# Hybrid decoder block: first weight parts of a group queued earlier, down inputs split in pieces, one weight ring to the end

## The chip, the cores and the metric

The kernel runs on one core of a Trainium2 chip. The metric is the device time of the whole program in microseconds (us). The core has a matrix engine (TensorE, PE in the profile; its weight loads are PEld), VectorE (DVE), ScalarE (ACT), GpSimd (POOL), and SyncE (SP), which here issues most of the DMA transfers.

## The reference, cut to what matters

One decoder block on 256 tokens of width 2048: a mixer (pooling beside differential attention), an output projection with a norm, then a dense SwiGLU feed-forward with D_FF = 5632, whose projections are the part that the change touches. All is float32.

```python
proj = rms_norm(h, pre_mix_norm) @ w_in
mixed = concat([pool_out, attn_out]) @ w_out
h = h + rms_norm(mixed, post_mix_norm)

hn = rms_norm(h, pre_ffn_norm)
ff = (silu(hn @ w_gate) * (hn @ w_up)) @ w_down
h = h + rms_norm(ff, post_ffn_norm)
```

## The kernel before, in words

**Precision.** Every float32 product is made of three matmuls in a reduced float32 format. Each operand is split into a high part (a rounding copy, on ACT) and a low part (operand minus high part, on DVE), and high x high, low x high and high x low are summed in PSUM. So each piece of weights that SP loads (`raw`) has to be split by one ACT instruction (`whi`, `wh`, `rh`) and one DVE instruction (`wlo`, `wl`, `rl`) before PE can use it in full.

**Feed-forward, first half.** The 5632 columns are done in 11 groups of 512 (index c). Group 0 is done with plain products: `w_g0`, then `w_u0`. Groups 1 to 10 are one loop. Its step j (0 to 7) takes a tile of 1 MB that holds two k-slices of w_up and of w_gate (`blocks`, two transfers). In steps j of `SK = (0, 2, 5)` the 2 x 2 blocks are multiplied with seven products in place of eight, which needs four sums of weight blocks: DVE makes `T` with three instructions (line 697), and `rh`, `rl`, `wh`, `wl` are the parts of the blocks and of the sums. The other steps only split the tile. Behind step 5 the banks m1, m5, m6 and m7 are combined into `s1`, `u2`, `u3`, `u4` (tag `cmb`, eight buffers in the pool `ft`). Behind step 7 come the evacuations: DVE makes `sg` from m2 and m4, ACT applies SiLU, DVE makes `u` from m3 and m8, and `gated` makes the two tiles `gg`. These are transposed on PE in `g_parts` of the next group (line 675, through one PSUM bank, tag `m5`) and copied to `gT[c]` by ACT (line 676).

**Down projection.** `closing` runs over four chunks of 512 output columns; each goes over k = 0 to 43 (tiles of four k, two halves of 512 KB). Its left operands are the split `gT`: `gh` on ACT (line 781), `gl` on DVE (line 782), one instruction each for a group's four k, made in chunk 0 ahead of k = 0, 4, 8 and so on. At the end of a chunk the sum of squares is taken on ACT and the gain is applied on DVE into a tile `mg`. In the last chunk the last eight k are held back and done for the first 128 tokens, then for the other 128. The residual `x` is read back from DRAM (`kept`).

**Memory.** The pools of the left and right side of the SBUF are stacks. The loop over groups has its weight ring `ring2` on the right (`raw` three tiles of 1 MB, `wh` and `wl` two, `rh` and `rl` two, `T` one). After the loop it closes `ring2`, the activations `acts`, `psum_m` and `ft`, and opens `last` and `ring3` in their place. `ring3` has six raw halves and five halves of each part.

**Order.** The program is written in the order of the source. A planner, when the program is built, runs its own model of time and hands each engine the instruction that the model finds ready; of several ready ones it takes the earlier in the source. `tc.issue_after(i)` keeps an instruction behind i on i's engine. On the chip every engine works through its list in the planned order and waits where an input is not ready. With `reuse_waits="tile"` a tile waits only for the tiles whose memory it takes over.

These lines stand around the change (before):

```python
gg = [gated(ps[t][:, :], t) for t in range(2)]      # group 0, ahead of the loop
...
raw = blocks(j)                                      # in step j of the loop
...
g_parts(NF // 4 - 1, gg)                             # behind the loop
p_ring2.close(); p_acts.close(); p_m.close(); p_ft.close()
...
before_k[0] = lambda c, i: g_split(i // 4) if c == 0 and i % 4 == 0 else None
```

Of the kernel before, what the change touches and what calls it, by code (L numbers as in the profile page):

```python
# [15 lines left out]
P = 128  # L16
S = 256
D = 2048
# [27 lines left out]
def block_kernel(ctx: ExitStack, tc: tile.TileContext, x, xT, pos, cols, rows, lamv, invf, invcnt,  # L46
# [4 lines left out]
    cp = ctx.enter_context(tc.tile_pool(name="cp", bufs=1))  # L51
    p_acts = ExitStack()
    acts = p_acts.enter_context(tc.tile_pool(name="acts", bufs=1, side="right"))
    p_ring = ExitStack()
# [10 lines left out]
    def small(shape, dt=F32, tag="tiny", bufs=24):  # L65
        return tiny.tile(shape, dt, tag=tag, name=nm(tag), bufs=bufs)
# [9 lines left out]

    def raw_tile():
        return ring.tile([P, 1024], F32, tag="raw", name=nm("raw"), bufs=RAW)
# [3 lines left out]
    def load(src, half):  # L82
        raw = raw_of[0]()
        latest[0] = sync.dma_start(raw, src[:, half * 1024:(half + 1) * 1024]).ins
        return raw
# [9 lines left out]
    parts_of = [lambda raw: ring_parts()]  # L95

    def split(raw, parts=None, by=None):
        hi, lo = parts() if parts else parts_of[0](raw)
        act.activation(hi, raw, AF.Copy)  # L99
        (by or dve).tensor_tensor(lo, raw, hi.bitcast(F32), ALU.subtract)  # L100
        return hi, lo
# [122 lines left out]

    pad = small([P, 8], tag="pad", bufs=1)
    pool.memset(pad, 0.0)
# [403 lines left out]
    ft = p_ft.enter_context(tc.tile_pool(name="ft", bufs=1, reuse_waits="tile"))  # L630
    p_m = ExitStack()
    psum_m = p_m.enter_context(tc.tile_pool(name="psum_m", bufs=1, space=bass.MemoryType.PSUM, reuse_waits="tile"))

# [23 lines left out]
    p_ring.close()  # L657
    p_ring2 = ExitStack()
    ring2 = p_ring2.enter_context(tc.tile_pool(name="ring2", bufs=1, side="right", reuse_waits="tile"))

    def gated(up, t):
        res = ft.tile([P, 512], F32, tag="gg", name=nm("gg"), bufs=3)
        dve.scalar_tensor_tensor(res, up, rstd3[:, t:t + 1], sg[t], ALU.mult, ALU.mult)
        return res

    gg = [gated(ps[t][:, :], t) for t in range(2)]

# [9 lines left out]

    def blocks(j):
# [22 lines left out]
    cmb = lambda name: ft.tile([P, 512], F32, tag="cmb", name=nm(name), bufs=CMB)  # L701

    for c in range(1, NF // 4):
        src = w_gu[c - 1]
        m = {1: bank(), 2: bank(), 3: bank(), 4: bank(), 5: None, 6: bank2(), 7: psum_m.tile([P, 512], F32, tag="m7", name=nm("m7"), bufs=1), 8: bank2()}
# [13 lines left out]

        for j in range(NKD // 2):  # L720
            raw = blocks(j)
            k1, k2 = 2 * j, 2 * j + 1
            if j in SK:
                if m[5] is None:
                    m[5] = m5_bank()
                s = ring2.tile([P, 4, 512], F32, tag="T", name=nm("T"), bufs=1)
                rh = high(raw[:, 1:4], "rh")
                tt(s[:, 0:2], raw[:, 1:3], raw[:, 0:1].to_broadcast([P, 2, 512]), ALU.add)
                tt(s[:, 2], s[:, 0], raw[:, 2], ALU.add)
                tt(s[:, 3], s[:, 2], raw[:, 3], ALU.add)  # L730
                rl = low(raw[:, 1:4], rh, "rl")
                sh = high(s, "wh")
                sl = low(s, sh, "wl")
                form = lambda i: (sums_h[j][:, i], sums_l[j][:, i])
                product(1, hh(k1, 0), rh[:, 0], rl[:, 0])
                product(3, form(3), rh[:, 1], rl[:, 1])
                product(2, hh(k2, 0), rh[:, 2], rl[:, 2])
                product(7, form(1), sh[:, 1], sl[:, 1])
                product(6, form(2), sh[:, 2], sl[:, 2])
                product(4, hh(k2, 1), sh[:, 3], sl[:, 3])  # L740
                product(5, form(0), sh[:, 0], sl[:, 0])
            else:
                wh = high(raw, "wh")
                wl = low(raw, wh, "wl")
# [12 lines left out]
        sg = [cp.tile([P, 512], F32, tag="gain", name=nm("sg"), bufs=2) for _ in range(2)]  # L757
        for t, (i, u) in enumerate(((2, s1), (4, u3))):
# [15 lines left out]
    raw_of[0] = lambda: ring3.tile([P, 1024], F32, tag="raw", name=nm("raw"), bufs=RAW)  # L774
    parts_of[0] = lambda raw: [ring3.tile([P, 1024], F32R, tag=f"w{z}", name=nm(f"w{z}"), bufs=5) for z in ("hi", "lo")]
    gh, gl = [], []

    def g_split(c):
        gh.append(last.tile([P, 4, 2, P], F32R, name=f"gh{c}"))
        gl.append(fp.tile([P, 4, 2, P], F32R, tag="g", name=f"gl{c}", bufs=NF // 4 + 1))  # L780
        act.activation(gh[c], gT[c], AF.Copy)
        dve.tensor_tensor(gl[c], gT[c], gh[c].bitcast(F32), ALU.subtract)

    mg_tile = lambda: last.tile([P, 512], F32, tag="mg", name=nm("mg"), bufs=8)
    for t in range(2):
        xn[t] = last.tile([P, D], F32, name=f"x{t}")
        load_after(xn[t], kept[t])
    f_k = (lambda k, t: gh[k // 4][:, k % 4, t, :], lambda k, t: gl[k // 4][:, k % 4, t, :])
    before_k[0] = lambda c, i: g_split(i // 4) if c == 0 and i % 4 == 0 else None

# [63 lines left out]
```

## Time and profile before

| | us |
|---|---|
| median of 3 runs | 1064.86 (1064.5 to 1066.73) |
| the profiled execution | 1064.52 |
| its span, first to last instruction | 1062.7 |
| PE busy | 1031.5 (97%) |
| DVE busy | 735.2 (69%) |
| ACT busy | 541.8 (51%) |
| mean granted clock of PE | 0.988 |

A row of a time line has the start in us from the span's start, the duration, the engine, the line of the source, the operation, output <- inputs with shapes, and the count where neighbours are merged; in square brackets stands the idle time of the engine before it and what ended it. A row of waits reads: who waited <- for whom: us in total, times, longest. A row of a costly group has, after the count, busy us and the mean in ns of one, then the idle time before them and what ended it. A row of transfers has the size of one and the us from issue to landing. A matmul's busy time overlaps with the next one's, so the spacing of starts tells its cost, not the mean of one.

### The profile page before, as it was taken

To read this page: it belongs to the slowest core of one execution; us is meant where nothing else is said; L and a number is where in the kernel's file an instruction comes from. 1 tells how busy PE (TensorE), PEld (TensorE's weight loads), DVE (VectorE), ACT (ScalarE), POOL (GpSimd) and SP (SyncE) were. 2 spreads that over 40 slices of the span, in tenths; PEclk is the share of its full clock that TensorE was granted. 3 is DMA by queue.
4 is the path that set the end of the run, shared out by engine and by line. 5 is a ranking of instruction groups with operands and counts; after the bars stand their busy time and mean duration, and the time that the engine had idled before them with its cause. 6 is when DMAs were issued, how large, how long until landed. Compare 5 with 4: busy or idle time off the path is not lost.

```text
span 1062.7 us, 12625 instructions
## 1 busy us (share of the span) xinstructions
PE 1031.5 (97%) x4787; PEld 846.2 (80%) x4787; DVE 735.2 (69%) x836; ACT 541.8 (51%) x632; POOL 35.1 (3%) x57
## 2 busy tenths in 40 slices
PE   8999999999999899999999999999986999999996
PEld 6789888988777688888888888888875888888885
DVE  6649755865677778888888788897867454444544
ACT  6746555654638455544555455555546343343431
POOL 0003100200030000000000000000000000000000
PEclk9999999999999899999999999999997999999999
DMA  8753554555755355665555555556537655655542
GB/s 330 279 175 131 180 179 160 166 188 192 253 191 179 113 197 185 206 212 177 197 198 198 198 198 183 202 191 216 179 129 276 213 194 188 199 196 192 197 139 79
DMA packets 57517, 203.39 MB, mean 191 GB/s; under 512 B 6896, under 2 KB 7792, under 8 KB 56688
## 3 DMA queue, kind: packets, MB, share of 16 engines
q1 hardware_dynamic: 57168, 202.44, 55.7%
q8 instruction: 37, 0.61, 0.2%
q14 instruction: 24, 0.20, 0.1%
q10 hardware_dynamic: 288, 0.15, 0.0%
HBM read 198.37 MB, written 4.19 MB: 191 GB/s over the span
## 4 chain that ended last, share of the span: by engine, by line
PE 87%; DVE 4%; DMA 4%; ACT 2%; issue 1%; SPq 0%; DVEq 0%; ACTq 0%
PE mm L136 14%; PE mm L135 14%; PE mm L137 14%; PE mm L716 8%; PE mm L718 8%; PE mm L717 8%; PE tr L717 3%; PE tr L716 3%; PE tr L718 3%; PE mm L171 2%; PE mm L173 1%; PE mm L172 1%; PE m L716 1%; PE m L717 1%; PE m L718 1%
## 5 line engine op out<-in xcount | busy, mean ns | idle before, releaser
L100 DVE TENSOR_TENSOR wlo<-raw,whi 128x1024 fp32r<-128x1024 f32 x185 | 226.7, 1227 | 190.8 <-ACT whi L99 184.3
L99 ACT ACTIVATE whi<-raw 128x1024 fp32r<-128x1024 f32 x185 | 195.0, 1058 | 212.4 <-PE mm L136 194.4
L135 PE MATMUL mm<-whi,gh 128*128 128x512 f32 x352 | 140.3, 399 | 2.7 <-ACT whi L99 2.7
L136 PE MATMUL mm<-whi,gl 128*128 128x512 f32 x352 | 140.5, 399 | 0.0
L137 PE MATMUL mm<-wlo,gh 128*128 128x512 f32 x352 | 137.1, 391 | 0.0
L717 PE MATMUL mm<-wh,h 128*128 128x512 f32 x330 | 129.4, 392 | 0.0
L716 PE MATMUL mm<-wh,h 128*128 128x512 f32 x330 | 129.3, 392 | 0.0
L688 DVE TENSOR_TENSOR wl<-raw,wh 128x2048 fp32r<-128x2048 f32 x50 | 114.3, 2286 | 6.7 <-ACT wh L693 6.7
L718 PE MATMUL mm<-wl,h 128*128 128x512 f32 x330 | 113.3, 393 | 0.0
L688 DVE TENSOR_TENSOR wl<-T,wh 128x2048 fp32r<-128x2048 f32 x30 | 68.7, 2289 | 54.7 <-ACT wh L693 54.7
L693 ACT ACTIVATE wh<-T 128x2048 fp32r<-128x2048 f32 x30 | 57.4, 1913 | 95.4 <-DVE T L697 69.3
L693 ACT ACTIVATE wh<-raw 128x2048 fp32r<-128x2048 f32 x50 | 95.4, 1908 | 13.7 <-issue 10.5
L135 PEld LDWEIGHTS mm<-whi,gh 128*128 128x128 f32 x352 | 66.6, 189 | 18.3 <-ACT whi L99 3.1
L137 PEld LDWEIGHTS mm<-wlo,gh 128*128 128x128 f32 x352 | 68.0, 193 | 15.6
L135 PE MATMUL mm<-whi,x 128*128 128x512 f32 x192 | 75.2, 396 | 3.0 <-ACT whi L277 1.9
L136 PEld LDWEIGHTS mm<-whi,gl 128*128 128x128 f32 x352 | 66.5, 189 | 13.8
L136 PE MATMUL mm<-whi,x 128*128 128x512 f32 x192 | 74.9, 393 | 0.0
L717 PEld LDWEIGHTS mm<-wh,h 128*128 128x128 f32 x330 | 62.1, 188 | 13.7
L716 PEld LDWEIGHTS mm<-wh,h 128*128 128x128 f32 x330 | 62.2, 189 | 13.4
L718 PEld LDWEIGHTS mm<-wl,h 128*128 128x128 f32 x330 | 62.0, 188 | 12.9
L137 PE MATMUL mm<-wlo,x 128*128 128x512 f32 x192 | 70.7, 393 | 0.1
L693 ACT ACTIVATE rh<-raw 128x1536 fp32r<-128x1536 f32 x30 | 44.5, 1485 | 25.2 <-DMA raw<-in_w_gu 25.1
(238 smaller groups left out, 1803.1 us busy)
## 6 DMA issues: line engine op xcount, KB each, us to landing
raw<-in_w_gu SPq DMA_DIRECT2D x160, 512.0 KB, 4.4
raw<-in_w_down SPq DMA_DIRECT2D x88, 512.0 KB, 3.6
raw<-in_w_in SPq DMA_DIRECT2D x46, 512.0 KB, 3.7
raw<-in_w_out SPq DMA_DIRECT2D x32, 512.0 KB, 3.6
raw<-in_w_u SPq DMA_DIRECT2D x24, 512.0 KB, 3.5
raw<-in_w_g SPq DMA_DIRECT2D x8, 512.0 KB, 6.1
xn<-in_x SPq DMA_DIRECT2D x2, 1024.0 KB, 9.3
gain<-in_rows SPq DMA_DIRECT2D x8, 256.0 KB, 3.9
```

The source lines that it names most:

```text
L99: act.activation(hi, raw, AF.Copy)
L100: (by or dve).tensor_tensor(lo, raw, hi.bitcast(F32), ALU.subtract)
L135: mm.matmul(ps[t][:, :], lhsT=a[0](k, t), rhs=wh, start=first, stop=False)
L136: mm.matmul(ps[t][:, :], lhsT=a[1](k, t), rhs=wh, start=False, stop=False)
L137: mm.matmul(ps[t][:, :], lhsT=a[0](k, t), rhs=wl, start=False, stop=last)
L171: mm.matmul(o, lhsT=wh, rhs=xh, start=st, stop=False)
L172: mm.matmul(o, lhsT=wh, rhs=xl, start=False, stop=False)
L688: dve.tensor_tensor(res, x, hi.bitcast(F32), ALU.subtract)
L693: act.activation(res, x, AF.Copy)
L716: mm.matmul(o, lhsT=a[0], rhs=wh, start=first, stop=False)
L717: mm.matmul(o, lhsT=a[1], rhs=wh, start=False, stop=False)
L718: mm.matmul(o, lhsT=a[0], rhs=wl, start=False, stop=left[i] == 0)
```

## The change

1. The work on a tile of step j is put into a function `prepare(c, j)`. The parts of step 0 of a group are made in the source ahead of the evacuations of the group before: `prepare(1, 0)` stands ahead of the two `gated` of group 0, and `prepare(c + 1, 0)` behind step 7 of group c, ahead of `sg`, SiLU, `u` and `gated`.
2. `ring2`, `acts` and `psum_m` stay open to the end. The down stage takes its raw halves and parts as halves of the ring's whole tiles (`raw` three, `wh` and `wl` two) and its `mg` tiles as thirds of `rh` and `rl`. Only `ft` is closed; `last` takes its place on the left, and `gg` moves to the pool `fp`.
3. `gh` and `gl` are made in pieces of two k. The first six `gh` pieces lie in `last`, the others in tiles of the activations; from c = 1 the ACT instruction is kept behind the last weight split ahead of it in the source. `g_parts` of the last group moves from behind the loop to ahead of k = 8 in chunk 0, and the loads of `x` from ahead of chunk 0 to the start of chunk 1.
4. `pad` grows from 32 to 160 bytes a partition.

The diff, cut to its core:

```diff
-    pad = small([P, 8], tag="pad", bufs=1)
+    pad = small([P, 40], tag="pad", bufs=1)
...
     def gated(up, t):
-        res = ft.tile([P, 512], F32, tag="gg", name=nm("gg"), bufs=3)
+        res = fp.tile([P, 512], F32, tag="gg", name=nm("gg"), bufs=3)
...
-    gg = [gated(ps[t][:, :], t) for t in range(2)]
...
+    def prepare(c, j):
+        raw = blocks(w_gu[c - 1], j)
+        if j not in SK:
+            wh = high(raw, "wh")
+            return wh, low(raw, wh, "wl")
+        s = ring2.tile([P, 4, 512], F32, tag="T", name=nm("T"), bufs=1)
+        rh = high(raw[:, 1:4], "rh")
+        tt(s[:, 0:2], raw[:, 1:3], raw[:, 0:1].to_broadcast([P, 2, 512]), ALU.add)
+        tt(s[:, 2], s[:, 0], raw[:, 2], ALU.add)
+        tt(s[:, 3], s[:, 2], raw[:, 3], ALU.add)
+        rl = low(raw[:, 1:4], rh, "rl")
+        sh = high(s, "wh")
+        return rh, rl, sh, low(s, sh, "wl")
+
+    ready = prepare(1, 0)
+    gg = [gated(ps[t][:, :], t) for t in range(2)]
     for c in range(1, NF // 4):
...
         for j in range(NKD // 2):
-            raw = blocks(j)
+            parts = ready if j == 0 else prepare(c, j)
...
             if j == SK[-1] + 1:
                 g_parts(c - 1, gg)
+        if c < NF // 4 - 1:
+            ready = prepare(c + 1, 0)
         sg = [cp.tile([P, 512], F32, tag="gain", name=nm("sg"), bufs=2) for _ in range(2)]
...
-    g_parts(NF // 4 - 1, gg)
-    p_ring2.close()
-    p_acts.close()
-    p_m.close()
     p_ft.close()
-    last = ctx.enter_context(tc.tile_pool(name="last", bufs=1, side="right", reuse_waits="tile"))
-    ring3 = ctx.enter_context(tc.tile_pool(name="ring3", bufs=1, side="right", reuse_waits="tile"))
-    raw_of[0] = lambda: ring3.tile([P, 1024], F32, tag="raw", name=nm("raw"), bufs=RAW)
-    parts_of[0] = lambda raw: [ring3.tile([P, 1024], F32R, tag=f"w{z}", name=nm(f"w{z}"), bufs=5) for z in ("hi", "lo")]
+    last = ctx.enter_context(tc.tile_pool(name="last", bufs=1, reuse_waits="tile"))
+    whole = {}
+    def of_whole(tag, dt, bufs):
+        def one(half=None):
+            h = whole.get((tag, "half"), 0) if half is None else half
+            if h == 0:
+                whole[tag] = ring2.tile([P, 4, 512], dt, tag=tag, name=nm(tag), bufs=bufs).rearrange("p a b -> p (a b)")
+            whole[tag, "half"] = 1 - h
+            return whole[tag][:, h * 1024:(h + 1) * 1024]
+        return one
+    raw_of[0] = of_whole("raw", F32, 3)
+    two = of_whole("wh", F32R, 2), of_whole("wl", F32R, 2)
+    parts_of[0] = lambda: (two[0](), two[1]())
     def g_split(c):
-        gh.append(last.tile([P, 4, 2, P], F32R, name=f"gh{c}"))
         gl.append(fp.tile([P, 4, 2, P], F32R, tag="g", name=f"gl{c}", bufs=NF // 4 + 1))
-        act.activation(gh[c], gT[c], AF.Copy)
-        dve.tensor_tensor(gl[c], gT[c], gh[c].bitcast(F32), ALU.subtract)
+        for half in range(2):
+            z = slice(2 * half, 2 * half + 2)
+            if c < 3:
+                gh.append(last.tile([P, 2, 2, P], F32R, name=f"gh{c}_{half}"))
+            else:
+                gh.append(half_tile("gh").rearrange("p (a b c) -> p a b c", a=2, b=2))
+            with tc.issue_after(last_split[0]) if c > 0 else nullcontext():
+                act.activation(gh[-1], gT[c][:, z], AF.Copy)
+            dve.tensor_tensor(gl[c][:, z], gT[c][:, z], gh[-1].bitcast(F32), ALU.subtract)
+
+    def before_down(c, i):
+        if c == 0 and i % 4 == 0:
+            if i == 8:
+                g_parts(NF // 4 - 1, gg)
+            g_split(i // 4)
+        if c == 1 and i == 0:
+            for t in range(2):
+                xn[t] = last.tile([P, D], F32, name=f"x{t}")
+                load_after(xn[t], kept[t])
-    for t in range(2):
-        xn[t] = last.tile([P, D], F32, name=f"x{t}")
-        load_after(xn[t], kept[t])
-    before_k[0] = lambda c, i: g_split(i // 4) if c == 0 and i % 4 == 0 else None
+    before_k[0] = before_down
```

More of the change, by code (lines that the diff above doesn't have):

```diff
@@ L51, in block_kernel @@
     cp = ctx.enter_context(tc.tile_pool(name="cp", bufs=1))
-    p_acts = ExitStack()
-    acts = p_acts.enter_context(tc.tile_pool(name="acts", bufs=1, side="right"))
+    acts = ctx.enter_context(tc.tile_pool(name="acts", bufs=1, side="right"))
     p_ring = ExitStack()
@@ L75, in block_kernel, with raw_tile @@
     latest = [None]
-    def raw_tile():
+    def raw_tile(half=0):
         return ring.tile([P, 1024], F32, tag="raw", name=nm("raw"), bufs=RAW)
@@ L82, in load @@
     def load(src, half):
-        raw = raw_of[0]()
+        raw = raw_of[0](half)
         latest[0] = sync.dma_start(raw, src[:, half * 1024:(half + 1) * 1024]).ins
@@ L93, in ring_parts @@
         return (ring.tile([P, 1024], F32R, tag=f"w{z}", name=nm(f"w{z}"), bufs=RING) for z in ("hi", "lo"))
-    parts_of = [lambda raw: ring_parts()]
+    parts_of = [ring_parts]
+    last_split = [None]
     def split(raw, parts=None, by=None):
-        hi, lo = parts() if parts else parts_of[0](raw)
-        act.activation(hi, raw, AF.Copy)
+        hi, lo = (parts or parts_of[0])()
+        last_split[0] = act.activation(hi, raw, AF.Copy).ins
         (by or dve).tensor_tensor(lo, raw, hi.bitcast(F32), ALU.subtract)
@@ L630, in block_kernel @@
     ft = p_ft.enter_context(tc.tile_pool(name="ft", bufs=1, reuse_waits="tile"))
-    p_m = ExitStack()
-    psum_m = p_m.enter_context(tc.tile_pool(name="psum_m", bufs=1, space=bass.MemoryType.PSUM, reuse_waits="tile"))
+    psum_m = ctx.enter_context(tc.tile_pool(name="psum_m", bufs=1, space=bass.MemoryType.PSUM, reuse_waits="tile"))
     sums_h, sums_l = {}, {}
@@ L657, in block_kernel @@
     p_ring.close()
-    p_ring2 = ExitStack()
-    ring2 = p_ring2.enter_context(tc.tile_pool(name="ring2", bufs=1, side="right", reuse_waits="tile"))
+    ring2 = ctx.enter_context(tc.tile_pool(name="ring2", bufs=1, side="right", reuse_waits="tile"))
     def gated(up, t):
-        res = ft.tile([P, 512], F32, tag="gg", name=nm("gg"), bufs=3)
+        res = fp.tile([P, 512], F32, tag="gg", name=nm("gg"), bufs=3)
         dve.scalar_tensor_tensor(res, up, rstd3[:, t:t + 1], sg[t], ALU.mult, ALU.mult)
         return res
-    gg = [gated(ps[t][:, :], t) for t in range(2)]
     def m5_bank():
@@ L676, in g_parts, with blocks @@
             act.activation(gT[c][:, :, t, :], tr.rearrange("p (a b) -> p a b", b=P), AF.Copy)
-    def blocks(j):
+    def blocks(src, j):
         raw = ring2.tile([P, 4, 512], F32, tag="raw", name=nm("raw"), bufs=3)
@@ L701, in block_kernel @@
     cmb = lambda name: ft.tile([P, 512], F32, tag="cmb", name=nm(name), bufs=CMB)
+    def prepare(c, j):
[13 more added lines that the diff above has]
+    gg = [gated(ps[t][:, :], t) for t in range(2)]
     for c in range(1, NF // 4):
-        src = w_gu[c - 1]
         m = {1: bank(), 2: bank(), 3: bank(), 4: bank(), 5: None, 6: bank2(), 7: psum_m.tile([P, 512], F32, tag="m7", name=nm("m7"), bufs=1), 8: bank2()}
@@ L725, in block_kernel @@
                     m[5] = m5_bank()
[L726 to L733, printed above, removed]
+                rh, rl, sh, sl = parts
                 form = lambda i: (sums_h[j][:, i], sums_l[j][:, i])
@@ L742, in block_kernel @@
             else:
-                wh = high(raw, "wh")
-                wl = low(raw, wh, "wl")
+                wh, wl = parts
                 for i, t, up in ((2, 0, 0), (4, 1, 0), (3, 0, 1), (8, 1, 1)):
@@ L776, in block_kernel @@
+    parts_of[0] = lambda: (two[0](), two[1]())
     gh, gl = [], []
     def g_split(c):
-        gh.append(last.tile([P, 4, 2, P], F32R, name=f"gh{c}"))
         gl.append(fp.tile([P, 4, 2, P], F32R, tag="g", name=f"gl{c}", bufs=NF // 4 + 1))
-        act.activation(gh[c], gT[c], AF.Copy)
-        dve.tensor_tensor(gl[c], gT[c], gh[c].bitcast(F32), ALU.subtract)
-    mg_tile = lambda: last.tile([P, 512], F32, tag="mg", name=nm("mg"), bufs=8)
-    for t in range(2):
-        xn[t] = last.tile([P, D], F32, name=f"x{t}")
-        load_after(xn[t], kept[t])
@@ L788, in block_kernel @@
-    f_k = (lambda k, t: gh[k // 4][:, k % 4, t, :], lambda k, t: gl[k // 4][:, k % 4, t, :])
-    before_k[0] = lambda c, i: g_split(i // 4) if c == 0 and i % 4 == 0 else None
+        for half in range(2):
[7 more added lines that the diff above has]
+            dve.tensor_tensor(gl[c][:, z], gT[c][:, z], gh[-1].bitcast(F32), ALU.subtract)
@@ new lines, in before_down, with mg_tile @@
+    def before_down(c, i):
[8 more added lines that the diff above has]
+    before_k[0] = before_down
+    mgs = []
+    def mg_tile():
+        n = len(mgs)
+        if used[0] == n:
+            three = ring2.tile([P, 3, 512], F32, tag="rh" if n % 2 == 0 else "rl", name=nm("mg"), bufs=2)
+            mgs.extend(three[:, i] for i in range(3))
+        used[0] += 1
+        return mgs[used[0] - 1]
@@ L791, in store @@
+    used = [0]
+    f_k = (lambda k, t: gh[k // 2][:, k % 2, t, :], lambda k, t: gl[k // 4][:, k % 4, t, :])
     def store(c, t, z):
```

## The prediction

> **What bounds the kernel now.** I read the profile's first two parts, then the waits of TensorE (PE), then tables of windows around each of its stalls, then the time lines of the engines that ended them.
>
> ```profile
> PE 1031.5 (97%) x4787; PEld 846.2 (80%) x4787; DVE 735.2 (69%) x836; ACT 541.8 (51%) x632; POOL 35.1 (3%) x57
> PEclk9999999999999899999999999999997999999999
> ```
>
> PE is busy 97% of the span: the 31 us in which it is not, and the stretches with a dip in the PEclk line (the 14th and the 31st slice, each 26.6 us wide), are all that a change of order can win.
>
> ```profile
> PE m L675 <- ACT gT L676: 9.3, 2, 8.6
> PE mm L135 <- ACT whi L99: 3.7, 2, 2.7
> PE mm L718 <- DVE rl L688: 3.0, 1, 3.0
> PE m L716 <- ACT wh L693: 1.0, 1, 1.0
> ```
>
> These are the waits near the change: 9.3 and 2.7 us where the feed-forward's last group hands over to the down projection, 3.0 and 1.0 us at the start of the first of the ten groups (c = 1). The windows give the price of both places. Columns: window, its length, busy time and count of PE, PEld, DVE, ACT, POOL, then the granted clock.
>
> ```profile
> 358.00:370.00 12.00, 8.00 (x25) 5.58 (x24) 9.92 (x9) 5.09 (x3) 0.00 (x0) 0.72 0.26 87
> 370.00:790.00 420.00, 419.88 (x1867) 344.22 (x1866) 351.47 (x288) 213.54 (x152) 0.00 (x0) 1.00 0.56 193
> 794.00:808.50 14.50, 2.51 (x11) 1.48 (x9) 7.90 (x9) 13.11 (x16) 0.00 (x0) 0.66 0.74 273
> 808.50:812.40 3.90, 3.89 (x9) 3.10 (x10) 3.90 (x4) 3.74 (x4) 0.00 (x0) 0.51 0.69 239
> 820.00:1050.00 230.00, 230.00 (x996) 188.32 (x996) 106.76 (x94) 90.48 (x96) 0.00 (x0) 1.00 0.54 180
> ```
>
> From 370 to 790 us, which holds all the later group boundaries, PE is busy 419.88 of 420.00 us: nothing can be won there. One matmul takes 230 / 996 = 0.231 us of a full stream. Between 794.0 and 808.5 PE works 2.51 us of 14.5, and after it the clock stays at 0.51 for 3.9 us more.
>
> **Part 1, the start of the down projection.** Why PE stands still there:
>
> ```profile
> 792.95 0.58 ACT L676 ACTIVATE gT<-m 128x512 f32<-128x512 f32 x1
> 793.71 8.63 ACT L781 ACTIVATE gh<-gT 128x1024 fp32r<-128x1024 f32 x9 [0.18 <-PE tr L717]
> 802.24 0.57 ACT L676 ACTIVATE gT<-m 128x512 f32<-128x512 f32 x1
> 802.87 1.11 PE L675 MATMUL m<-ident,gg 128*128 128x128 f32 x4 [8.59 <-ACT gT L676]
> 804.67 1.12 PE L675 MATMUL m<-ident,gg 128*128 128x128 f32 x4 [0.69 <-ACT gT L676]
> 807.42 4.83 ACT L99 ACTIVATE whi<-raw 128x1024 fp32r<-128x1024 f32 x5
> 808.51 0.80 PE L135 MATMUL mm<-whi,gh 128*128 128x512 f32 x1 [2.72 <-ACT whi L99]
> 793.64 0.33 SPq L90 DMA_DIRECT2D x<-kept  x1
> 794.91 18.56 SPq L84 DMA_DIRECT2D raw<-in_w_down  x9
> ```
>
> Nine `gh` splits stand in ScalarE's list ahead of a 0.57 us copy of the one bank that the transposes share; the transposes of line 675 wait 8.59 us for it, and the first down matmul waits behind them. The down weights are not there earlier either: SP issues them from 794.91 us on, behind the two loads of `x`.
>
> The change takes all of this away. The weights stay in the one ring, so their loads and splits run on as between groups. What the first matmul needs is two pieces of `gh` (0.58 us each, by the 128x512 copy above) and two of `gl`. Their slots in the new pool lie where combination buffers of earlier groups were, and ACT has room for them:
>
> ```profile
> 791.41 0.73 ACT L760 ACTIVATE sg<-sg,rstd 128x512 f32<-128x512 f32 x1 [7.92 <-DVE sg L697]
> ```
>
> ACT stood idle 7.92 us just before 791.41, while the last products ran. The last group's transposes move to k = 8, where 8 x 6 matmuls x 0.231 = 11.1 us of down work cover the gating that they wait for.
>
> The sum: idle 14.50 - 2.51 = 12.0 us; nine matmuls in 3.90 us instead of 9 x 0.231 = 2.1, so 1.8; two blocks of four transposes at the low clock, 1.11 and 1.12 us, against 0.60 for a block at full clock, 1.0:
>
> ```profile
> 793.68 0.60 PE L675 MATMUL m<-ident,gg 128*128 128x128 f32 x4
> ```
>
> Together 14.8 us. I put 0.7 back: the second block still waits for the copy of the first out of the single bank, the 0.69 in the row above, now in the middle of chunk 0. Bounds of this rest are 0 (a block with matmuls between, as in all groups up to 790 us) and 5.6 (the second rival). Net 14.1.
>
> **Part 2, pieces and ring in the down stage.** Per weight tile of four k, PE needs 24 x 0.231 = 5.5 us. The other engines' prices:
>
> ```profile
> L100 DVE TENSOR_TENSOR wlo<-raw,whi 128x1024 fp32r<-128x1024 f32 x185 | 226.7, 1227 | 190.8 <-ACT whi L99 184.3
> L99 ACT ACTIVATE whi<-raw 128x1024 fp32r<-128x1024 f32 x185 | 195.0, 1058 | 212.4 <-PE mm L136 194.4
> raw<-in_w_down SPq DMA_DIRECT2D x88, 512.0 KB, 3.6
> 404.95 0.69 DVE L697 TENSOR_TENSOR sg<-mm,s 128x512 f32<-128x512 f32 x1 [0.40 <-PE mm L718]
> ```
>
> A `gh` piece costs ACT 0.58 and a `gl` piece DVE 0.69 (an operation on 128x512, the last row), so in chunk 0 ACT has 2 x 1.06 + 2 x 0.58 = 3.3 us a tile and DVE 2 x 1.23 + 2 x 0.69 = 3.8, both under 5.5. The ring now frees parts by whole tiles, two of them, where five halves stood. From one tile's release to both halves split is 1.06 + 1.23 + 1.23 = 3.5 us, again under the 5.5 us that the other tile lasts. The tight place is the last chunk, whose eight held k fill both tiles: PE then needs the second tile after 12 matmuls, 2.8 us, its first half is ready after 1.06 + 1.23 = 2.3. Cost 0, at most 3.5 - 2.8 = 0.7 once; if the cover of 5.5 us is lost, each tile costs up to 3.5. The two `x` loads leave SP's queue ahead of the first down weights (a gain counted above) and stand in chunk 1 ahead of weight loads: 2 MB at the 273 GB/s of the window row at 794 is 7.7 us, and with 3.6 to land 11.3, against two tiles of cover, 11.0. Cost 0, bounds 0 and 2. Squares and gains at chunk ends keep their work; their tiles now lie in the ring. The pad moves the left tiles by 128 bytes; splits on the left (after 808 us) and on the right (before 360 us) share one mean of 1.227 us, so I take 0, bounds -1 and +1.
>
> **Part 3, the first parts ahead of the evacuations.** The instructions stay the same; DVE's order may change. In later groups it hardly can:
>
> ```profile
> 395.87 1.22 DVE L697 TENSOR_TENSOR T<-raw 128x1024 f32<-128x1024 f32 x1
> 406.47 2.28 DVE L688 TENSOR_TENSOR wl<-T,wh 128x2048 fp32r<-128x2048 f32 x1
> 408.67 0.69 DVE L697 TENSOR_TENSOR u<-mm,u 128x512 f32<-128x512 f32 x1
> ```
>
> The next group's first sum `T` runs 9 us before the `sg` of 404.95 although the program has it after: the planner issues what its model finds ready, and program order only breaks ties. With `T` go its two loads on SP, which has no other transfer there, and `rh` and `wh` on ACT; POOL has no part in it. So nine boundaries: 0. In the first group it is otherwise:
>
> ```profile
> 352.21 1.48 ACT L693 ACTIVATE rh<-raw 128x1536 fp32r<-128x1536 f32 x1
> 357.64 1.51 DVE L663 SCALAR_TENSOR_TENSOR gg<-mm,rstd,sg 128x512 f32<-128x512 f32 x2 [3.99 <-PE mm L137]
> 359.07 1.22 DVE L697 TENSOR_TENSOR T<-raw 128x1024 f32<-128x1024 f32 x1
> 360.93 1.75 DVE L688 TENSOR_TENSOR rl<-raw,rh 128x1536 fp32r<-128x1536 f32 x1
> 362.59 0.69 DVE L697 TENSOR_TENSOR T<-T,raw 128x512 f32<-128x512 f32 x1
> ```
>
> The weights were in place at 352.21 (`rh` read them), yet `T` stood behind the two `gg`, which waited 3.99 us for PE. With `T` first, 358 to 370 us would shrink from 12.0 to 25 x 0.231 = 5.8: 6.2 us. But DVE was idle in the plan as well, and `T` was not taken: the planner believed the weights not yet landed when `gg` became ready, and nothing in the change brings that load forward. A tie-break does not help one that is not ready. I take 0, with bounds 0 and -6.2, the nearer row being `gg` ahead of `T`.
>
> **Sum.** The profiled execution took 1064.5 us (span 1062.7 and 1.8 around it), 0.3 under the median of 1064.86. 1064.5 - 14.1 = 1050.4 us.
>
> **Rivals.** (1) Slower: at each of nine boundaries VectorE does the next group's first parts as a block before the evacuations. T, two more sums, `rl`, `wl` are 1.22 + 0.69 + 0.69 + 1.75 + 2.28 = 6.6 us, of which the 2.28 already stands between `sg` and `u`. So 4.3 us more before `u` frees the bank for the next group: 9 x 4.3 = 39 us, 1050.4 + 39 = 1089. It decides from 14.1 / 9 = 1.6 us a boundary. Against it: `T` is 9 us ahead already. 0.08.
> (2) Half kept: the first `gl` piece waits on VectorE behind the last `gg`, which ended at 795.96:
>
> ```profile
> 795.21 0.75 DVE L663 SCALAR_TENSOR_TENSOR gg<-u,rstd,sg 128x512 f32<-128x512 f32 x1
> ```
>
> Then PE waits from 793.7 to 796.6, 2.9 us, and as in the first group (6.2 lost for 4.0 waited) some 2.0 more at the low clock: 4.9 in place of 0, 1055.3 (with the 0.7, 5.6 for the rest). 0.12.
> (3) Both: the planner takes `T` first in the first group, 1050.4 - 6.2 = 1044.2. 0.18.
> (4) No change: the stall is given back, the copies of line 676 again behind splits; 1064.5. 0.04.
>
> [...]
>
> **How the numbers follow.** My forecast, 1048 to 1053, has 0.58. The range from 1043 to 1057 holds it with rivals 3 and most of 2, some 0.85, and leaves 1 and 4 out. What a measurement can tell from no change is about 0.2%, 2.1 us: faster 0.58 + 0.12 + 0.18 = 0.88, same 0.04, slower 0.08.
>
> **What would show it.** Right: no wait of PE on `gT` above 1 us; no dip of the clock near 794 us; down matmuls within 1 us of the last group's; w_down loads before 790 us. `gg` still ahead of `T` near 358 us says part 3 is right, `T` ahead says rival 3. Wrong would be PE waits at 370 to 790 us (rival 1), or L135 waiting for `whi` throughout the down stage (part 2).

## The result and the profile after

The changed kernel takes 1049.01 us (median of 4 runs, 1048.25 to 1050.27) where the kernel before took 1065.80 in the runs beside it (4 runs, 1064.5 to 1066.98). The ratio is 0.9844, 95% interval 0.9827 to 0.9861. The forecast was 1050.4 us. The time agrees with it, but mostly because errors cancel: the start of the down stage gave about 8.7 us where 14.1 were counted, the end of the kernel lost 2.1 us where at most 0.7 were counted, and the pad, counted at nothing, gave 8.7. This section shows where the time went, the experiments show which part did it.

The profiled execution took 1049.04 us, with a span of 1047.2. First the lines of the profile's page that answer to those of before:

```profile
PE 1021.4 (98%) x4787; PEld 843.5 (81%) x4787; DVE 732.1 (70%) x847; ACT 537.5 (51%) x643; POOL 34.6 (3%) x57
PEclk9999999999999899999999999999998999999998
```

PE does the same 4787 matmuls in 10.1 us less busy time (1021.4 against 1031.5). Taking out idle time cannot do that, and the low clock that went with it was worth only some 3 us (1.8 and 1.0 in the prediction). It is the first sign that the matmuls themselves became shorter.

The waits of PE in the changed kernel, those near the change (total, count, longest):

```profile
PE mm L731 <- DVE rl L685: 3.0, 1, 3.0
PE m L672 <- DVE wl L100: 2.0, 1, 2.0
PE m L729 <- ACT wh L690: 1.6, 1, 1.6
PE mm L136 <- DVE gl L803: 1.2, 1, 1.2
PE mm L137 <- DVE wlo L100: 0.2, 1, 0.2
```

The 9.3 us on `gT` and the 2.7 us on `whi` are gone. In their place stand 2.0 us ahead of a block of transposes (the profile names `wl`; the rows further down show that it is a copy to `gT` again) and 1.2 us (on `gl`, the first down piece). The 3.0 us of the first group stay. No wait above 0.2 us stands at the nine later boundaries, and none on the weights' high parts in the down stage.

The table divides both profiled spans at the same five marks, start times of matmuls in the two time lines. The column in the middle is the first experiment, the kernel before with only the new pad.

| stretch, us | before | before + pad | after |
|---|---|---|---|
| start to first product of group 1 | 358.12 | 355.93 | 356.77 |
| to the last product of group 10 | 435.33 | 433.68 | 432.61 |
| to the first down matmul (handover) | 15.06 | 15.06 | 3.31 |
| to the last down matmul | 245.65 | 240.76 | 243.86 |
| to the end | 8.57 | 8.56 | 10.69 |
| span | 1062.73 | 1053.99 | 1047.24 |

So the pad gives 8.74 us (2.2 before the groups, 1.65 in them, 4.89 in the down stage). All the rest gives 6.75: 11.75 at the handover, less 3.10 in the down stage behind it and 2.13 at the end, and 0.23 net ahead of the handover. Each column is one execution. The first stretch holds the first loads and takes 355.7 to 357.0 us in the eight traces with the pad of 160 bytes and 357.2 to 361.1 in the five with another, so its 2.2 is certain to a us or so only. The 4.89 rests on the pace of the matmuls, shown below.

The handover in the time lines of the changed kernel, PE first (start, duration, and in brackets the idle time before and its releaser):

```profile
789.38 0.39 PE L731 MATMUL tr<-wl,h 128*128 128x512 f32 x1
789.61 0.60 PE L672 MATMUL m<-ident,gg 128*128 128x128 f32 x4
792.17 0.66 PE L672 MATMUL m<-ident,gg 128*128 128x128 f32 x4 [1.96 <-DVE wl L100]
792.69 0.73 PE L135 MATMUL mm<-wh,gh 128*128 128x512 f32 x2
794.62 0.80 PE L136 MATMUL mm<-wh,gl 128*128 128x512 f32 x1 [1.21 <-DVE gl L803]
795.22 0.63 PE L137 MATMUL mm<-wl,gh 128*128 128x512 f32 x1
```

Then DVE and ACT:

```profile
789.68 0.75 DVE L661 SCALAR_TENSOR_TENSOR gg<-u,rstd,sg 128x512 f32<-128x512 f32 x1
790.95 1.22 DVE L100 TENSOR_TENSOR wl<-raw,wh 128x1024 fp32r<-128x1024 f32 x1
792.09 0.74 DVE L661 SCALAR_TENSOR_TENSOR gg<-u,rstd,sg 128x512 f32<-128x512 f32 x1
792.75 1.22 DVE L100 TENSOR_TENSOR wl<-raw,wh 128x1024 fp32r<-128x1024 f32 x1
793.88 2.49 DVE L803 TENSOR_TENSOR gl<-gT,gh 128x512 fp32r<-128x512 f32 x4
```

```profile
783.67 2.01 ACT L99 ACTIVATE wh<-raw 128x1024 fp32r<-128x1024 f32 x2 [4.20 <-PE tr L730]
789.63 2.00 ACT L99 ACTIVATE wh<-raw 128x1024 fp32r<-128x1024 f32 x2
791.54 0.58 ACT L673 ACTIVATE gT<-m 128x512 f32<-128x512 f32 x1
792.02 2.18 ACT L802 ACTIVATE gh<-gT 128x512 fp32r<-128x512 f32 x4
```

The first `gh` pieces were not split in ACT's idle time ahead of the boundary, such as the 4.20 us before 783.67. They stand at 792.02, behind the last products. So the first `gl` comes at 793.88, behind the last `gg` and a `wl` on DVE, and PE waits for it.

The four transposes at 792.17 are the first of the last group's two blocks; those at 789.61 are still of group 9, since the last group's first `gg` only starts at 789.68. What the block at 792.17 waits 1.96 us for is not `wl`: the transposes do not read it, and it ends at 790.95 + 1.22 = 792.17, the very moment of their start. They need the one bank that all transposes share, and the copy of line 673 that empties it ends at 791.54 + 0.58 = 792.12, 0.05 us before them; in the kernel before, the copy at 802.24 ended 0.06 us before the transposes at 802.87. The copy at 791.54 stood on ACT behind two weight splits (789.63, 2.00 us). So the bank's wait of before is still there, at 1.96 us in place of 8.59. The two waits cost the clock too:

```profile
786.00:790.00 4.00, 4.00 (x23) 3.29 (x21) 3.33 (x5) 2.24 (x4) 0.00 (x0) 1.00 0.53 156
793.40:800.30 6.90, 5.70 (x15) 4.46 (x14) 2.97 (x5) 1.39 (x3) 0.00 (x0) 0.51 0.40 152
801.00:1030.00 229.00, 229.00 (x1014) 189.60 (x1013) 114.21 (x110) 99.27 (x117) 0.00 (x0) 1.00 0.56 192
```

In these windows (length, busy time and count of PE, PEld, DVE, ACT, POOL, then the granted clock) the clock is 0.51 for 6.9 us from 793.4 on, and 1.00 before the handover and after it. What a stall costs in clock differs from execution to execution: with the first group's 3.0 us wait the mean clock from 356 to 372 us is 0.79 before and 0.89 in this trace, but 0.79 again with the early `gh` of an experiment below, which leaves that part as it is. The last section has the low stretches beside the waits.

The end, on ACT, before and after:

```profile
1049.04 0.60 ACT L534 ACTIVATE sqj<-mm 128x512 bf16<-128x512 f32 x1 [7.49 <-PE mm L137]
1054.59 0.60 ACT L534 ACTIVATE sqj<-mm 128x512 bf16<-128x512 f32 x1 [4.38 <-PE mm L137]
```

```profile
1034.94 0.60 ACT L534 ACTIVATE sqj<-mm 128x512 bf16<-128x512 f32 x1 [7.05 <-PE mm L137]
1036.98 0.60 ACT L534 ACTIVATE sqj<-mm 128x512 bf16<-128x512 f32 x1 [0.87 <-PE mm L137]
1040.06 0.20 ACT L195 ACTIVATE tiny<-tiny 128x1 f32<-128x1 f32 x1 [2.39 <-DVE tiny L188]
```

The squares of the two token halves stood 5.55 us apart and now stand 2.04 apart. So the first half's closing on DVE no longer lies under the second half's matmuls, and the second half's closing waits for it: ACT sits idle 2.39 us before the row at 1040.06.

### The profile page after: what moved, and what is told of

The parts are those of the page before. It is cut to its first block, busy times and chain, and to the rows that moved or that the text cites. A ratio compares the mean times of both kernels' runs of the same rounds, so it can differ in the third digit from the quotient of the medians.

```text
span 1047.2 us, 12568 instructions
## 1 busy us (share of the span) xinstructions
PE 1021.4 (98%) x4787; PEld 843.5 (81%) x4787; DVE 732.1 (70%) x847; ACT 537.5 (51%) x643; POOL 34.6 (3%) x57
## 4 chain that ended last, share of the span: by engine, by line
PE 88%; DVE 6%; DMA 3%; issue 2%; ACT 1%; SPq 0%; DVEq 0%; ACTq 0%
PE mm L137 15%; PE mm L136 15%; PE mm L135 15%; PE mm L729 8%; PE mm L731 8%; PE mm L730 8%; PE tr L730 2%; PE tr L729 2%; PE tr L731 2%; DMA raw<-in_w_gu 2%; PE mm L171 2%; PE mm L173 1%; PE mm L172 1%; DVE xn L561 1%; PE m L729 1%
## 5 line engine op out<-in xcount | busy, mean ns | idle before, releaser
L100 DVE TENSOR_TENSOR wl<-raw,wh 128x1024 fp32r<-128x1024 f32 x88 | 104.7, 1222 | 112.9 <-ACT wh L99 112.9
L100 DVE TENSOR_TENSOR wlo<-raw,whi 128x1024 fp32r<-128x1024 f32 x97 | 119.2, 1229 | 70.4 <-ACT whi L99 64.0
L99 ACT ACTIVATE wh<-raw 128x1024 fp32r<-128x1024 f32 x88 | 89.3, 1052 | 128.0 <-PE mm L136 123.8
L99 ACT ACTIVATE whi<-raw 128x1024 fp32r<-128x1024 f32 x97 | 102.2, 1057 | 78.1 <-PE mm L136 60.7
L136 PE MATMUL mm<-wh,gl 128*128 128x512 f32 x352 | 138.2, 393 | 1.2 <-DVE gl L803 1.2
L135 PE MATMUL mm<-wh,gh 128*128 128x512 f32 x352 | 136.3, 392 | 0.0
L137 PE MATMUL mm<-wl,gh 128*128 128x512 f32 x352 | 131.4, 392 | 0.0
L136 PEld LDWEIGHTS mm<-wh,gl 128*128 128x128 f32 x352 | 66.7, 190 | 15.5 <-DVE gl L803 1.6
L137 PEld LDWEIGHTS mm<-wl,gh 128*128 128x128 f32 x352 | 66.8, 190 | 14.1
L135 PEld LDWEIGHTS mm<-wh,gh 128*128 128x128 f32 x352 | 66.5, 189 | 13.9
```

What stands on the lines that cost most here:

```text
L99: last_split[0] = act.activation(hi, raw, AF.Copy).ins
L135: mm.matmul(ps[t][:, :], lhsT=a[0](k, t), rhs=wh, start=first, stop=False)
L136: mm.matmul(ps[t][:, :], lhsT=a[1](k, t), rhs=wh, start=False, stop=False)
L137: mm.matmul(ps[t][:, :], lhsT=a[0](k, t), rhs=wl, start=False, stop=last)
```

## Experiments

Each run's ratio is to the kernel before, run on the same chip beside it: 1065.95 us with the first four kernels, 1064.97 with the next four, 1066.33 with the last three. Kernels are compared by these ratios.

**The pad alone.** The kernel before with the one line of the pad changed:

```
-    pad = small([P, 8], tag="pad", bufs=1)
+    pad = small([P, 40], tag="pad", bufs=1)
```

> The kernel before with the pad of 160 bytes alone. In the kernel before, the start-to-start time of matmuls was 227 ns where both operands lie at the same SBUF address modulo 256 (weights at 224, activations at 224, and the held weights at 96 with mh and ml at 96) and 232 to 234 ns where one lies at 224 and the other at 96 (mh, ml, sh, sl, gl against weights of the right side); in the changed kernel all is at 224 and 227 ns. Theory A: the pad alone removes this. From the counts of such pairs (some 700 with gl x 6.7 ns, 300 with mh and ml x 5.2 ns, 330 with sh and sl x 6 ns): 4.7 + 1.6 + 2.0 = 8.3 us less than the kernel before, 1057.5 us, and 227 ns in all pairs. Rival: the new places of the weights in one ring and the pieces of gh made the difference; then this run stays at the time of the kernel before, 1065.8 +- 1, with 232 ns still in the down stage.

Measured: 1056.09 us (4 runs, 1054.38 to 1056.72), ratio 0.9908 (0.9895 to 0.9920). The pad alone gives 0.9%, 9.9 us by the medians. The window from 820 to 1020 us, deep in the down stage, shows how. Before, with the pad, and after:

```profile
820.00:1020.00 200.00, 200.00 (x867) 163.75 (x867) 96.10 (x84) 81.29 (x86) 0.00 (x0) 1.00 0.60 198
```

```profile
820.00:1020.00 200.00, 200.00 (x884) 165.68 (x883) 95.82 (x84) 83.21 (x88) 0.00 (x0) 1.00 0.61 201
```

```profile
820.00:1020.00 200.00, 200.00 (x884) 165.59 (x883) 98.79 (x94) 84.76 (x100) 0.00 (x0) 1.00 0.60 209
```

PE is busy all the 200 us in each, at full clock, without a wait. Before, it does 867 matmuls there (230.7 ns each), with the pad 884 (226.2 ns), after the whole change 884 again. So in these three traces the matmul rate of the down stage goes with the pad, and neither the new ring nor the pieces nor the `x` loads touch it.

The pad only moves tiles; the order of the instructions on each engine is the same with all pads. In the program before, the tiles on the right side of SBUF (weights and their parts, `h`, `gh`) start at 224 modulo 256 bytes, those on the left (`mh`, `ml`, `sh`, `sl`, `gl`) at 96. With 128 bytes more in the pad the left ones start at 224 too. From start to start, the trace of before gives 227 ns (median) where the two operands agree (`whi,x` and `wh,h`, both at 224, and `hhi,mh`, both at 96), and 232 to 234 where one of two matmuls in turn has operands 128 bytes apart: `whi,gh` to `whi,gl` 232, `whi,gl` to `wlo,gh` 234, but `wlo,gh` to `whi,gh` 227. In the trace of after the same down-stage intervals are 226 to 227.

**The other sizes of the pad.** Four kernels vary only the pad of the changed kernel:

```
-    pad = small([P, 40], tag="pad", bufs=1)
+    pad = small([P, 8], tag="pad", bufs=1)     # 32 bytes; in the others 72 (288), 24 (96), 32 (128)
```

With 32 bytes:

> The changed kernel with the old pad of 32 bytes. Theory A (address phase of the two operands modulo 256): mh, ml, sh, sl, gl and six of the gh pieces fall back to 96 against weights at 224; 8.3 us slower than the changed kernel, 1057.3 us, and 232 to 234 ns at those pairs again. Rival (ring and pieces): 1049.0 +- 1 and 227 ns.

With 288 bytes:

> The changed kernel with a pad of 288 bytes, 128 more. Theory A, modulo 256: the left side is at 96 again, as with 32 bytes, so 1057.3 us. Rival B, that any larger distance from the small tiles helps, or that the period is 128 or less: 1049.0. If the period were 512 or more, this place would be a new one, neither that of 32 nor of 160 bytes, and the time could lie anywhere between.

With 96 bytes:

> The changed kernel with a pad of 96 bytes: left tiles at 160 modulo 256 against 224 on the right, a distance of 64. Theory A with a half-and-half rule (same half of 256 bytes or not): a matmul's rows of 2 KB cross both halves at every distance, so a distance of 64 should cost something between 0 and the 5 to 7 ns of 128; linear in the distance that is half, 4.2 us, 1053.2. If only the distance of 128 is bad: 1049.0.

With 128 bytes:

> Changed kernel with the pad of 128 bytes instead of 160: the left operands (mh, ml, gh, gl and the like) then start 32 bytes away from the right ones, modulo 256. If any difference of the two addresses modulo 256 costs its 2 to 6 ns a product: 1056 to 1058 us, like the pads of 96 and 32 bytes. If only the place in units of 64 bytes counts and 192 and 224 are one unit: 1049.0 us.

| pad, bytes | left tiles modulo 256 | away from 224 | median us (runs) | ratio, interval | count in the window |
|---|---|---|---|---|---|
| 32 | 96 | 128 | 1057.97 (6) | 0.9929, 0.9912 to 0.9947 | 865 |
| 288 | 96 | 128 | 1057.17 (5) | 0.9917, 0.9904 to 0.9929 | 865 |
| 96 | 160 | 64 | 1056.82 (4) | 0.9915, 0.9903 to 0.9928 | 866 |
| 128 | 192 | 32 | 1058.56 (5) | 0.9925, 0.9911 to 0.9938 | 865 |
| 160 (the change) | 224 | 0 | 1049.01 (4) | 0.9844, 0.9827 to 0.9861 | 884 |

The last column is PE's count in the window 820 to 1020. The row with 32 bytes of distance has as few matmuls as the ones with 128:

```profile
820.00:1020.00 200.00, 200.00 (x865) 161.98 (x864) 97.50 (x95) 83.81 (x99) 0.00 (x0) 1.00 0.59 204
```

The pad of 288 bytes is 128 more than the fast one and has 865 matmuls, so it is not the amount of memory, and equal places modulo 128 are not enough. In the changed kernel `gl` and the weights lie 256 bytes apart modulo 512, and the pairs with `gl` still take 226 to 227 ns, so equal places modulo 512 are not needed. Of the pads that were run, only the one that brings both sides to the same place modulo 256 has 884 matmuls in the window, in the kernel before as in the changed one: 226.2 ns each (200 / 884), against 230.7 to 231.2 (200 / 867 and 200 / 865) with all others. Distances of 32 and 64 bytes cost about as much as 128 (865 and 866 against 865), so both guesses that a small distance costs less fell (1053.2 for the linear one; 1049.0 for units of 64 bytes). Why the place matters is not settled: no view shows what PE waits for inside a matmul.

**The first `gh` pieces in slots of their own.** Why did `gh` come late? The six tiles of `last` lie where the group loop's pool `ft` was. By the addresses in the program, the two pieces for k = 0 to 3 take over buffers of group 9, whose last readers are that group's two `gg`, at 750.81 and 753.67 us. So their own memory was free some 38 us early, and on the chip the first piece even starts before the last group's last `gg` (792.02 against 792.09). What puts them late is their place in ACT's list: the plan has them behind the last reader of any tile of `ft`. This kernel puts the two pieces for k = 0 to 3 into the pool of `gT`, in slots that nothing else uses:

```
-            if c < 3:
+            if c == 0:
+                gh.append(fp.tile([P, 2, 2, P], F32R, tag="gh0", name=f"gh{c}_{half}", bufs=2))
+            elif c < 3:
```

> The changed kernel with one place of its own for the two gh pieces of k = 0 to 3 (in the pool fp instead of last), so that they can be split at any time once gT is there. Theory H: in the changed kernel the first down matmuls still wait because the planner lists these pieces only after the tiles of ft are done, behind the last evacuations (PE waits of 2.0 and 1.2 us, then 6.8 us at the low clock). With the pieces early the waits go and the clock holds: 2.0 + 1.2 + 6.83 x 0.5 x 0.9 = 6.2 us less than the changed kernel, 1042.8 us, no dip of the clock near 795 us. Rival: the wait is for the last group's gating whatever comes first, the next late input (the transposes or the first weight parts) takes its place: 1048 to 1050.

Measured: 1042.89 us (4 runs, 1041.68 to 1043.36), ratio 0.9792 (0.9779 to 0.9805), 0.0052 under the change. The summary of the `gh` instructions on ACT, first after, then here (duration minimum, median, maximum; first and last start):

```profile
L802 ACT ACTIVATE gh<-gT x22: 613/615/617, 792.0 to 847.8; 128x512 fp32r<-128x512 f32 x22
```

```profile
L804 ACT ACTIVATE gh<-gT x22: 612/615/636, 414.3 to 841.9; 128x512 fp32r<-128x512 f32 x22
```

With slots of their own the planner places the first piece at 414 us, as soon as group 0's `gT` is there. On PE the gap at the handover is gone:

```profile
789.80 0.39 PE L731 MATMUL tr<-wl,h 128*128 128x512 f32 x1
790.02 0.62 PE L135 MATMUL mm<-wh,gh 128*128 128x512 f32 x2
790.48 0.39 PE L136 MATMUL mm<-wh,gl 128*128 128x512 f32 x1
```

```profile
790.00:801.00 11.00, 11.00 (x54) 9.08 (x53) 9.59 (x12) 7.23 (x11) 0.00 (x0) 1.00 0.52 184
```

Full clock through 790 to 801, PE busy for all of it, and the transposes of the last group (line 672) end among down products, the last of them at 804.2. From the last product to the last down matmul it is 0.22 + 240.60 = 240.82 us, against 15.06 + 240.76 = 255.82 in the kernel before with the new pad: 15.0 us, the size that the prediction worked out for a clean handover (14.8, of which 0.7 were put back). Against the changed kernel the same stretch (3.31 + 243.86) is 6.35 us shorter, and the ratios give 5.5, for the 6.2 expected. That the plan opens `last` as a whole only when `ft` is done is inferred from the order of its lists; no view shows the planner's reason.

**The first group's order.** Here the two `gg` of group 0 are kept behind the split of the first raw input of group 1 (`rl`), to price the wait that part 3 left standing:

```
+        last_low[0] = last_dve[0]          # the instruction of rl in prepare(1, 0)
...
-    gg = [gated(ps[t][:, :], t) for t in range(2)]
+    with tc.issue_after(last_low[0]):
+        gg = [gated(ps[t][:, :], t) for t in range(2)]
```

> The changed kernel with the two gg of group 0 held behind rl of the first prepared tile in VectorE's list. Theory L: moving the lines in the source did nothing, the list order is what costs; with T and rl done while the last products of w_u0 run, the waits of 3.0 and 1.6 us and the low clock of 3.4 us at the start of the first group go: 3.0 + 1.6 + 1.5 = 6.1 us less than the changed kernel, 1042.9 us. Rival: gg, now later, holds the bank that the second product needs, and the wait comes back there: 1048 to 1050.

Measured: 1044.27 us (4 runs, 1041.86 to 1046.17), ratio 0.9805 (0.9787 to 0.9824), 0.0039 or 4.2 us under the change, for the 6.1 expected. The four runs lie 4.3 us apart, so the medians give this gain only roughly; in the profiled execution the stretch from the first product of group 1 to the last of group 10 takes 427.66 us against 432.61, 4.95 less. DVE around it, after and here:

```profile
356.29 1.43 DVE L661 SCALAR_TENSOR_TENSOR gg<-mm,rstd,sg 128x512 f32<-128x512 f32 x2 [3.83 <-PE mm L137]
357.64 1.22 DVE L694 TENSOR_TENSOR T<-raw 128x1024 f32<-128x1024 f32 x1
359.50 1.75 DVE L685 TENSOR_TENSOR rl<-raw,rh 128x1536 fp32r<-128x1536 f32 x1
```

```profile
351.28 1.22 DVE L696 TENSOR_TENSOR T<-raw 128x1024 f32<-128x1024 f32 x1
353.14 1.75 DVE L685 TENSOR_TENSOR rl<-raw,rh 128x1536 fp32r<-128x1536 f32 x1
355.18 1.43 DVE L661 SCALAR_TENSOR_TENSOR gg<-mm,rstd,sg 128x512 f32<-128x512 f32 x2 [0.29 <-PE mm L137]
```

`T` could have run at 351, as the prediction said: the weights were there, only DVE's list stood in the way. The wait of 3.0 us on `rl` is gone and the clock keeps 1.00 from 356 to 372 us (0.89 after), but two waits on `wh`, 1.6 us together, stay, about what is missing to 6.1.

The move of the preparation itself has no run of its own, because it changes nothing: without it the program has the same instructions in the same order on each engine, at the same addresses.

**The end: room or order?** Two theories for the 2.1 us. First, that the eight held k fill both whole tiles of the ring, so that the eighth is late and the last products mix; with six held there is room:

```
-    closing(lambda c: [w_down[c, i] for i in range(NF // 4)], f_k, NF, rows[1], None, 8,
+    closing(lambda c: [w_down[c, i] for i in range(NF // 4)], f_k, NF, rows[1], None, 6,
```

> The changed kernel with six held k in the last down chunk instead of eight. Theory E: with two whole tiles in the ring the eighth held k is late, so the matmuls of the two token halves interleave at the end, the squares of the halves are 2.0 us apart instead of 5.6, and the first half's closing is no longer hidden: the end after the last matmul grew from 8.6 to 10.7 us. Six held k leave the ring one half tile of room; 6 x 3 x 0.227 = 4.1 us between the halves, and the end is 8.6 again: 2.0 us less than the changed kernel, 1047.0 us. Rival: the end is set by the stores alone: 1049.0.

Measured: 1048.50 us (4 runs, 1047.9 to 1049.25), ratio 0.9847 (0.9833 to 0.9860). No gain. The squares are still 2.04 apart:

```profile
1034.33 0.60 ACT L534 ACTIVATE sqj<-mm 128x512 bf16<-128x512 f32 x1 [7.05 <-PE mm L137]
1036.37 0.60 ACT L534 ACTIVATE sqj<-mm 128x512 bf16<-128x512 f32 x1 [0.87 <-PE mm L137]
```

Room was the wrong theory. Second, that the planner's list mixes the two halves, because in its model products of the second half are ready while the first half still lacks a weight part. This kernel keeps the second half's held matmuls behind the first half's (`behind[0]` is the instruction that the kernel keeps its next matmuls behind):

```
                     for n, (i, k, wh, wl) in enumerate(held):
-                        mm_a(ps, a, t, k, wh, wl, i == 0, i == nk - 1)
+                        at = mm_a(ps, a, t, k, wh, wl, i == 0, i == nk - 1)
                         hook(t, n)
+                    if nk == NF:
+                        behind[0] = at
```

> Changed kernel, with one rule of order added: in the last down chunk the held products of the second token half are issued behind the last held product of the first half. Theory E2 (the 2.1 us that the end lost come from the written order, which mixes the two halves, not from a lack of slots): the two squares stand 24 products x 0.227 = 5.4 us apart instead of 2.04, the first half's closing lies under the second half's products again, and the end stands 8.6 us behind the last product instead of 10.69: -2.1, 1046.9 us. Rival (the order was mixed because the last w_down half is not split in time): the last wl split ended near 1029.3 and the first half now reads it at about 1029.8 to 1030.2, so TensorE waits there for VectorE, up to 1 to 2 us, and the median stays within 0.5 of 1049.0.

Measured: 1047.57 us (4 runs, 1045.52 to 1049.29, two near each end), ratio 0.9823 (0.9805 to 0.9840), 0.0021 or 2.2 us under the change. The intervals overlap, so the gain rests on the trace:

```profile
1030.15 0.60 ACT L536 ACTIVATE sqj<-mm 128x512 bf16<-128x512 f32 x1 [3.65 <-PE mm L137]
1035.59 0.60 ACT L536 ACTIVATE sqj<-mm 128x512 bf16<-128x512 f32 x1 [4.27 <-PE mm L137]
```

The squares are 5.44 apart, PE shows no wait in the last chunk, and from the start of the last matmul (1035.16) to the end (1043.73) it is 8.57 us, exactly as before the change. The order was the cause. That the planner's model is late with the last parts is inferred, not shown. On the chip they were in time.

**All together.** The three edits together, first with six held k, then with eight held k and the order:

> The three edits (gh pieces of the first k in a place of their own, gg behind rl, six held k) together in the changed kernel. Theories H, L and E all right and independent: 6.2 + 6.1 + 2.0 = 14.3 us less, 1034.7 us. If the rivals of all three hold: 1049.

> Changed kernel with three edits together: the first down chunk's gh pieces in slots of their own, the first group's SiLU product behind the split of the first raw input, and the held products of the two halves in order in the last down chunk (eight held pairs, not six). If the three lie at different places and add: 1042.9 - 4.8 - 2.1 = 1036.0 us, against 1037.8 with the six held pairs. Rival: as in the run with the order alone, the last split is late, and it stays at 1037.5 to 1038.5.

Measured: 1037.82 us (5 runs, 1037.35 to 1039.3), ratio 0.9746 (0.9733 to 0.9759), and 1037.66 us (4 runs, 1035.76 to 1038.47), ratio 0.9728 (0.9714 to 0.9742). The single differences to the change add up to 0.0112 (0.0052 + 0.0039 + 0.0021), and 0.9844 - 0.0112 = 0.9732 against 0.9728: within the intervals the three add. (In the second's profiled execution PE also waits 2.8 us for `rh`, at four places in the groups, where the change had 0.2; why is not shown.) The first fell short of its 1034.7 by 4.0 us by the ratio (0.9746 x 1065.8 = 1038.7), as its parts did alone: 2.0 at the end, 1.9 in the first group and 0.7 at the handover. The second beats both kernels, by 2.7% and 1.2%. Its page:

```profile
PE 1017.5 (98%) x4787; PEld 840.4 (81%) x4787; DVE 732.6 (71%) x847; ACT 537.7 (52%) x643; POOL 34.6 (3%) x57
```

## Why the prediction was right, and where it was not

**What bounds it: right.** All that was won lies in idle time and low clock at the handover, and in the matmul's own pace. The second was in the page before (230 / 996 = 0.231 us for a matmul of the down stage) and was read as the price of a matmul, though PE's time line of before has 0.227 in the groups (starts at 787.99, 788.22, 788.45 and 788.67 us). The two paces were not compared.

**Part 1, half right.** That the nine `gh` splits ahead of the copy and the loads behind `x` go away is right. SP's down weights are issued from 770 us, before the 790 asked for:

```profile
770.39 17.56 SPq L83 DMA_DIRECT2D raw<-in_w_down  x8
841.01 0.91 SPq L89 DMA_DIRECT2D x<-kept  x2
```

The step that failed is "Their slots in the new pool lie where combination buffers of earlier groups were, and ACT has room for them". On the chip both halves hold: the memory was free from about 754 us on, and ACT had room. But the plan lists the pieces behind the last group's gating, and `gh` came at 792.02. "The last group's transposes move to k = 8" failed with it for one of the two blocks: it ran at 792.17, ahead of the down products, and only the second moved, to 807.81. "The change takes all of this away" failed for the shared bank, whose copy again stood behind weight splits (1.96 us). Rival 2, the first `gl` behind the last `gg` on DVE, came with a wait of 1.21 us for the 2.9 that it gave.

The price was larger than the waits: the handover and the low clock behind it gave 11.75 - 3.10 = 8.65 us instead of 14.1, so 5.45 us were lost where rival 2 had 4.9. With early slots the step's own size is right: 15.0 measured against 14.8.

**Part 2, three terms.** The `x` loads and the ring cost nothing per tile: 884 matmuls in 200 us with them and without. "Cost 0, at most 3.5 - 2.8 = 0.7 once", for the last chunk, failed: it cost 2.13, and not through the ring's release but because the planned order mixed the two halves. The forecast priced a wait and did not look at the order in which the held products are handed out. The pad's term, "so I take 0, bounds -1 and +1", failed by most: -8.7 in the spans, -9.9 in the medians. The row that it was argued from has one mean for DVE's splits, 1.227 us; by the program's addresses their tiles start at 224 modulo 256 bytes in both stretches, so it could not show what a move costs. And it said nothing on PE, whose matmuls have a left and a right tile as inputs (`whi,gl`).

**Part 3: right at 0**: the move in the source leaves every engine's list as it was. That the planner's model takes the weights for not yet landed, the reason given, is not shown. `gg` still stands ahead of `T` (356.29 and 357.64) and the 3.0 us wait stays. Rival 3's 6.2 us is more than the order gives when it is forced: 4.2 by the medians, 4.95 in the trace.

**Rivals.** (1) is out: no wait above 0.2 us at 370 to 790 us. (4), the copies again behind splits, came true in small: 1.96 us in place of 8.59, so the stall was not given back. In this trace DVE and ACT kept to their planned lists, not to the source's order: `gl` at 793.88 stands behind a `gg` and a `wl`, and the copy to `gT` at 791.54 behind two weight splits (789.63, 2.00 us).

**The sum.** -14.1 was forecast. Measured in the spans: -8.74 (pad) - 8.65 (handover and the clock behind it) + 2.13 (end) - 0.23 (ahead of the handover) = -15.49. Of "what would show it", three signs came true (weights before 790, `gg` ahead of `T`, no waits in the groups). Three did not: PE still waits 1.96 us on a copy to `gT`, the clock still dips, from 793.4 us, and the first down matmul starts 3.3 us after the last product, not within 1. These three, read in the trace, tell more than the total does. That the total lay so near the forecast is luck.

## What to carry to other kernels

A total that comes out right proves no term of its sum: divide both spans at the same marks and check every term against its own stretch. Where PE is busy without a gap and still does fewer matmuls in a window than elsewhere, compare its start-to-start time by operand pair, and try another pad ahead of one side's tiles; here one line of padding, which brought both sides to 224 modulo 256 bytes, was worth 0.9%. Do not take the profile's name for what ended a wait on trust when that instruction ends at the same moment: ask what the waiting instruction reads and writes. Where a planner orders the work, early work needs a place in its plan as well as free memory and idle engines, and an order that matters at the end of the kernel has to be written down.

## What the runs showed of the hardware

A matmul of 128x512, medians from start to start: in the trace of before, where the left tiles lie 128 bytes from the right ones modulo 256, `whi,gh` to `whi,gl` takes 232 ns, `whi,gl` to `wlo,gh` 234, and the groups' `wh,sh` to `wh,sl` 241. In the trace of after, where both sides lie at 224, the like pairs (`wh`, `wl` and `gh`, `gl` in the names there; `wh,sh` to `wh,sl`) take 227, 226 and 227. With left tiles 32, 64 or 128 bytes away PE does 865 to 867 matmuls in the window from 820 to 1020 us, at the same place 884, at a granted clock of 1.00 in each. Over this kernel that is 7.6 to 9.9 us, by the runs above.

The clock, in the traces named, beside the waits of PE:

| place | in the trace of | waits of PE, us | granted clock |
|---|---|---|---|
| first group | before | 3.04, 1.0 | 0.50 from 361.74 to 368.56 us |
| first group | after | 3.01, 1.64 | 0.50 from 363.33 to 366.74 |
| first group | early `gh` | 3.0, 1.6 | 0.79 over 356 to 372 |
| first group | `gg` behind `rl` | 1.6 in two | 1.00 over 356 to 372 |
| handover | before | 12.0 idle of 14.50 from 794.0 | 0.50 from 798.65 to 812.29 |
| handover | after | 1.96, 1.21 | 0.50 from 793.41 to 800.24 |
| handover | early `gh` | none | 1.00 over 790 to 801 |

These rows do not show what sets the length of a low stretch: two like waits of about 3.0 us have 6.8 us of it before and 3.4 after. They do show what a short wait cost here: at the handover the waits of 1.96 and 1.21 us came with 6.83 us at 0.50 of the clock, in which PE worked 5.62 us. By an estimate from that row (half of 5.62) another 2.8 us were lost, nearly as much as the 3.2 us of the waits.
